# A two-layer encoder trunk on one core: 1488 of its 512-column products read their columns in another order

## The chip, the cores and the metric

The kernel runs on one core of a Trainium2 chip. The metric is the device time of one execution in microseconds (us), smaller is better. The engines are named as in the profile: PE is the matrix engine, PEld its weight loads, DVE the vector engine, ACT the scalar engine, POOL the general engine, SP the engine that issues most transfers. A PE product has a stationary operand of 128 by 128 values (its weight load) and a moving operand of 128 partitions by up to 512 columns, and it adds into a bank of 512 fp32 columns in PSUM.

## The reference

The reference is a trunk of two layers over 512 tokens of width 1024, batch 1, in float32. Layer A mixes by a matrix memory (4 heads) beside memory cross-attention, layer B by banded attention (12 heads) beside memory cross-attention. Each layer ends in an output projection and a gated MLP with a causal convolution. What bears on the change are these three places, in both layers:

```python
x = x + jnp.concatenate([mix_out, mem_out], axis=-1) @ w_out
u, g = jnp.split(h @ w_up, 2, axis=-1)          # D_FF = 2816 each
g = causal_dwconv(g, conv_w, conv_b)
return (jax.nn.silu(g) * u) @ w_down
```

The weights and the input are float32, and the result must agree with the float32 reference.

## The kernel before

Activations lie feature-major: a tile holds 128 features on the partitions and all 512 tokens on its columns. Every float32 operand is split into a high part (rounded to the fast fp32r type, by ACT, L140) and a low part (the rest, by DVE, L141). One float32 product of 128 by 128 weights with 512 tokens is three PE products, made by `mm3` (L192 to L196): high weights with high tokens, high weights with low tokens, low weights with high tokens, all into one PSUM bank. Since `mm3` records them, nearly all products of the kernel carry the lines L194, L195 and L196 in the profile, and the tiles tell them apart: `pmm`, `psc` and `ptr` are PSUM banks of the three tags "mm", "sc" and "tr" (3, 3 and 2 banks), `u` are tiles of 512 columns that hold split activations, `wh` and `wl` the split weights, `fh` and `fl` split forms of the weights in the MLP.

Weight tiles come from `weight_tiles` (L160). Two of its three pairs of buffers are 16 columns (`HALF`) longer than 1024, and one tile of such a pair begins 16 columns into its buffer (L167 to L171).

The products that the change touches are of 512 columns each, and contiguous in the columns before it:

- `project` (L198) makes one tile of 128 output features from 8 input tiles, so 24 PE products. It is called from many places; the change gives an order only to the calls in `ChannelMixer.plain` (L757), the gate and the up half of the first `PLAIN` = 5 tiles of each MLP: 5 tiles by 2 halves by 24 products by 2 layers = 480. The gate goes to a `pmm` bank, the up half to `psc`.
- `OutProjection.part` (L695) adds a few of the 8 mixed tiles at a time into 3 `pmm` banks and 2 banks of another tag (`ptr` in layer A, `psc` in layer B), as filler beside the last heads of the mixers: 5 banks by 8 tiles by 3 products by 2 layers = 240. The other 3 output tiles are made by `project` in `finish` (L708) and stay as they are.
- `ChannelMixer.down_products` (L822) multiplies one group of `GROUP` = 4 hidden tiles into one 128-row piece of the MLP's output, in a `ptr` bank: 32 pieces by 12 products by 2 layers = 768. ACT copies the bank to SBUF (L833) and a POOL transfer adds it to the spilled residual in DRAM (L834).

After the 5 plain tiles, each remaining MLP tile is made by `step` (L882) from seven blocks of products with 256 columns (`products`, L847), and its order on PE, ACT and DVE is written out by hand; up to two calls of `down_products` stand in one step. In the mixers, `weave` (L225) interleaves a job (a head of attention) with a filler (projections), at a rate written beside each call.

Of the kernel before, what the change touches and what calls it, by code (L numbers as in the profile page):

```python
# [16 lines left out]
P = 128  # L17
D = 1024
S = 512
KT = D // P  # L20
# [7 lines left out]
DFF = 2816  # L28
# [14 lines left out]
PLAIN, UNSCALED, GROUP, LAST = 5, 3, 4, 6  # L43
# [11 lines left out]
def trunk(  # L55
# [34 lines left out]
    def sb(tag, shape, dtype=F32):  # L90
        count[0] += 1
        return pool.tile(shape, dtype, tag=tag, name=f"{tag}{count[0]}", bufs=bufs[tag])

    def ps(tag):
        count[0] += 1
        return psum.tile([P, S], F32, tag=tag, name=f"p{tag}{count[0]}", bufs=pbufs[tag])
# [88 lines left out]
    def weights(*args):  # L185
        return parts(load(*args))

    def rows(w, c0, n, k0=0, k1=None):
        k1 = k1 if k1 is not None else w.shape[0] // P
        return w[k0 * P : k1 * P, c0 : c0 + n].rearrange("(k p) c -> p k c", p=P)  # L190

    def mm3(o, lh, ll, rh, rl, first, last, more=False):  # L192

        nc.tensor.matmul(o, lh, rh, start=first, stop=False, skip_group_check=more)  # L194
        nc.tensor.matmul(o, lh, rl, start=False, stop=False, skip_group_check=more)  # L195
        nc.tensor.matmul(o, ll, rh, start=False, stop=last, skip_group_check=more)  # L196

    def project(w, c0, act, tag="mm"):  # L198


        n = len(act)
        wh, wl = weights(rows(w, c0, P), n, P)
        o = ps(tag)
        for k in range(n):
            mm3(o, wh[:, k, :], wl[:, k, :], act[k][0], act[k][1], k == 0, k == n - 1)
            yield
        return o

    def run(gen):
        while True:  # L210
            try:
                next(gen)
            except StopIteration as end:
                return end.value

    def chain(*gens):
        for g in gens:
            yield from g

    def pair_of(a, b):  # L220
        first = yield from a
        second = yield from b
        return first, second

    def weave(job, filler, each, lead=0):  # L225

        due = lead
        for n in chain([0], job):
            due += each if n is None else each * n
            while due >= 1:  # L230
                due -= 1
                next(filler, None)
# [43 lines left out]
    class Norm:  # L276


        def __init__(self):
            self.acc = self.row = None  # L280
# [110 lines left out]
    def value_products_by_parts(os_, wh, wl, k0):  # L391

        n = wh.shape[1]
        for part, w in ((0, wh), (1, wh), (0, wl)):
            for k in range(n):
                for m, o in enumerate(os_):
                    a = memT[k0 + k][part][:, m * P : (m + 1) * P]
                    first = k0 + k == 0 and part == 0 and w is wh
                    nc.tensor.matmul(o, a, w[:, k, :], start=first, stop=w is wl and k0 + k == KT - 1)
# [63 lines left out]
    with tc.manual_schedule(engines={mybir.EngineType.PE, mybir.EngineType.Activation, mybir.EngineType.DVE}):  # L463

        logarithms()
        w = ps("mm")
# [39 lines left out]
        first, second = slice(0, MEM), slice(MEM, S)  # L506
# [13 lines left out]
        for q in range(KT // 2):  # L520
            k = 2 * q
# [166 lines left out]
    class OutProjection:  # L688


        def __init__(self, w, mixes, *groups):
            self.w, self.mixes, self.o = w, mixes, {}
            self.groups, self.n = groups, [0] * len(groups)

        def part(self, g, *ks):  # L695
            j0, j1, tag = self.groups[g]
            if j0 not in self.o:
                self.o.update((j, ps(tag)) for j in range(j0, j1))
            cols = slice(j0 * P, j1 * P)
            wh, wl = weights([self.w[k * P : (k + 1) * P, cols] for k in ks], len(ks), (j1 - j0) * P)  # L700
            for i, k in enumerate(ks):
                self.n[g] += 1
                for j in range(j0, j1):
                    c = slice((j - j0) * P, (j - j0 + 1) * P)
                    mm3(self.o[j], wh[:, i, c], wl[:, i, c], *self.mixes[k], self.n[g] == 1, self.n[g] == KT)
                    yield

        def finish(self, gnames):  # L708
# [12 lines left out]
    class ChannelMixer:  # L721
# [35 lines left out]
        def plain(self, j):  # L757
            scale = self.norm.row if j < UNSCALED else None
            act = self.act if j < UNSCALED else self.ready
            gate = project(self.w, DFF + j * P, act)  # L760
            up = project(self.w, j * P, act, "sc")
            if self.norm.row is None:
                both = pair_of(gate, up)
                weave(self.norm.finish(), both, 1)
                og, ou = yield from both
                scale = self.norm.row
            else:
                og = yield from gate
                ou = None
            acc = sb("t", [P, S])  # L770
            src = og
            if scale is not None:
                src = sb("t", [P, S])
                V.tensor_tensor(out=src, in0=og, in1=scale, op=ALU.mult)
            self.last_tap(j, acc, src)
            for _ in self.taps(j, acc, src):
                pass
            A.activation(acc, acc, AF.Silu)
            if scale is not None:
                V.tensor_mul(acc, acc, scale)  # L780
            if ou is None:
                ou = yield from up
            V.tensor_tensor(out=acc, in0=ou, in1=acc, op=ALU.mult)
            self.keep(acc)
# [37 lines left out]
        def down_products(self, u):  # L822
            g, j = divmod(u, KT)
            w = self.down[u // 2]
            o = ps("tr")
            c = slice(u % 2 * P, (u % 2 + 1) * P)
            for k in range(GROUP):
                mm3(o, w[0][:, k, c], w[1][:, k, c], *self.hid[GROUP * g + k], k == 0, k == GROUP - 1)
            return j, o

        def add(self, j, o):
# [211 lines left out]
    act = acts  # L1043
# [6 lines left out]
    def value_columns(hf):  # L1050
        n = AW // 2
        os_ = [ps(t) for t in ("mm", "mm", "mm", "sc")]
        for u in range(4):
            if hf:

                wh, wl = vw.pop()
                for j in range(2 * u + 2, min(2 * u + 4, KT)):
                    if j < KT - 1:
                        x_scaled(j + 1)
                    x_low(j)  # L1060
                    if j == 2 * u + 2:
                        vw.append(parts(value_weights(1, u + 1), pinned=True))
            else:
                wh, wl = parts(value_weights(0, u))
            nn = wh.shape[-1]
            for i in range(2):
                k = 2 * u + i
                for T in range(TT):
                    lh, ll = (t[:, T * P : (T + 1) * P] for t in act[k])
                    mm3(os_[T][:, :nn], lh, ll, wh[:, i, :], wl[:, i, :], k == 0, k == KT - 1)  # L1070
                    yield
        for T in range(TT):
            if hf:
                V.tensor_add(gt[:, T, :], os_[T][:, n : n + 8], gateb)
            hi, lo = sb("u", [P, S], F32R), sb("u", [P, S], F32R)
            G.memset(f(hi)[:, DH : DH + P], 1.0)
            G.memset(f(lo)[:, DH : DH + P], 0.0)
            split(pair(hi), pair(lo), os_[T][:, :n].rearrange("p (a b) -> p a b", a=2))
            vh[hf][T], vl[hf][T] = hi, lo
# [3 lines left out]
    e, u, c, r = (cpool.tile([P, TT, AH], F32, name=f"gate{i}") for i in range(4))  # L1083
# [7 lines left out]
    order = [(h, s) for h in range(AH) for s in range(TT)]  # L1091
# [80 lines left out]
    mixes = [None] * KT  # L1172
# [114 lines left out]
                mixes[j] = sb("u", [P, S], F32R), sb("u", [P, S], F32R)  # L1287
            split(mixes[j][0][r, :], mixes[j][1][r, :], og[j][r, :])

    outp = OutProjection(a_w_out, mixes, (0, 3, "mm"), (3, 5, "tr"))  # L1290
    run(value_columns(1))
    load_vectors(1)
    load_vectors(2)
# [44 lines left out]
    norm2, kvact, act = Norm(), [], []  # L1338
    for j in range(KT):
        wh, wl = weights(rows(ffn_w_down[0], j * P, P, FT - LAST, FT), LAST, P)  # L1340
        o = ps("mm")
# [10 lines left out]
    mixes = [None] * KT  # L1352
# [94 lines left out]
    def b_memory_queries(hp):  # L1447
        memq[hp] = queries((yield from project(b_w_in, AW + hp * P, act)), norm.row)

    qkv = {}  # L1450
    outp = OutProjection(b_w_out, mixes, (0, 3, "mm"), (3, 5, "sc"))
    fill = chain(*(project_pair(j) for j in range(5)), b_memory_queries(0), project_pair(5), b_memory_queries(1))
    weave(norm.finish(), fill, 1)
    for j in range(4):
# [65 lines left out]
    n = LAST // 2  # L1520
    for hf in range(2):
        os_ = [ps(t) for t in (("mm", "mm", "mm", "sc") if hf == 0 else ("sc", "sc", "tr", "tr"))]
        ws = [None] * n
        groups = [(range(TT), (slice(0, S),))]
        if hf:

            groups = [((0, 1), (slice(0, S),)), ((2,), (slice(0, S),)), ((3,), (slice(0, MEM), slice(MEM, S)))]
        for Ts, pieces in groups:
            for c in pieces:
                if c.start:  # L1530
                    os_[Ts[0]] = ps("mm")
                for u in range(n):
# [3 lines left out]
                    wh, wl = ws[u]  # L1536
                    for T in Ts:
                        for i in range(2):
                            k = 2 * u + i
                            lh, ll = (t[:, T * P : (T + 1) * P] for t in hid[k])  # L1540
# [57 lines left out]
```

## Time and profile before

| | us |
|---|---|
| median of 2 runs | 1178.32 |
| lowest and highest run | 1177.98, 1178.65 |
| span of the profiled execution | 1177.3 |
| PE busy (share) | 1167.7 (99%) |
| PEld busy (share) | 1033.3 (88%) |
| DVE busy (share) | 940.7 (80%) |
| ACT busy (share) | 728.5 (62%) |
| POOL busy (share) | 129.2 (11%) |

The span runs from the first to the last instruction of the profiled execution. A product's busy time in the profile overlaps the next product's, because products are pipelined; how often PE can start one is read from the start times in the timeline, not from the busy times. A group in the list of groups gives line, engine, operation, tiles and shapes, its count, its busy time in us and the mean of one in ns.

### The profile page before, as it was taken

How to read it: one execution, taken by the hardware profiler on the slowest of the kernel's cores; microseconds unless marked ns; L12 is line 12 of the kernel's file. 1: busy time of each engine (PE TensorE's matmuls, PEld its weight loads, DVE VectorE, ACT ScalarE, POOL GpSimd, SP SyncE). 2: the span in 40 equal slices, each digit the busy share in tenths (PEclk: the TensorE clock that was granted, in tenths of full speed). 3: DMA queues.
4: the chain of work that ended last, by engine and by line, in shares of the span. 5: the costliest groups of instructions: out<-in, count | busy, mean ns of one | idle time of the engine just before them, and what ended most of it. 6: DMA issues, size and time to landing. Idle time of an engine off the chain costs nothing.

```text
span 1177.3 us, 18645 instructions
## 1 busy us (share of the span) xinstructions
PE 1167.7 (99%) x7005; PEld 1033.3 (88%) x7005; DVE 940.7 (80%) x1680; ACT 728.5 (62%) x1297; POOL 129.2 (11%) x222
## 2 busy tenths in 40 slices
PE   9999999999999999999999999999999999999997
PEld 9988888888889999999888888778889999999986
DVE  6777788887979888777688888897897887777755
ACT  6548677655656655666666677676565666666545
POOL 1211101000021111111020000101001011110100
PEclk9999999999999999999999999999999999999999
DMA  8645325243366766665563312335426456666551
GB/s 277 230 111 140 86 55 152 76 144 116 90 159 159 181 166 165 167 147 118 154 204 117 90 54 89 112 89 179 142 90 152 108 138 142 143 144 144 126 161 72
DMA packets 199277, 158.64 MB, mean 135 GB/s; under 512 B 8361, under 2 KB 178063, under 8 KB 199187
## 3 DMA queue, kind: packets, MB, share of 16 engines
q1 hardware_dynamic: 183026, 119.74, 34.5%
q0 software_dynamic: 15584, 36.67, 15.6%
q8 instruction: 55, 0.90, 0.3%
q10 hardware_dynamic: 576, 1.05, 0.2%
q14 instruction: 36, 0.29, 0.1%
HBM read 128.89 MB, written 32.46 MB: 137 GB/s over the span
## 4 chain that ended last, share of the span: by engine, by line
PE 95%; ACT 2%; DVE 2%; issue 0%; POOL 0%; POOLq 0%; DVEq 0%; ACTq 0%
PE pmm L194 18%; PE pmm L195 18%; PE pmm L196 18%; PE ptr L195 6%; PE ptr L194 6%; PE ptr L196 6%; PE psc L196 5%; PE psc L195 5%; PE psc L194 5%; PE psc L600 2%; PE ptr L1421 1%; PE ptr L1442 1%; PE ptr L1443 1%; PE ptr L669 0%; PE pmm L491 0%; PE pmm L470 0%
## 5 line engine op out<-in xcount | busy, mean ns | idle before, releaser
L194 PE MATMUL pmm<-u,wh 128*128 128x512 f32 (+1 forms) x968 | 333.2, 345 | 0.2 <-ACT u L140 0.2
L196 PE MATMUL pmm<-u,wl 128*128 128x512 f32 (+1 forms) x968 | 330.6, 342 | 0.0
L195 PE MATMUL pmm<-u,wh 128*128 128x512 f32 (+1 forms) x968 | 330.4, 342 | 0.0
L141 DVE TENSOR_TENSOR wl<-wr,wh 128x1024 fp32r<-128x1024 f32 (+3 forms) x172 | 199.7, 1162 | 82.4 <-ACT wh L140 80.9
L140 ACT CAST wh<-wr 128x1024 fp32r<-128x1024 f32 (+3 forms) x172 | 171.9, 1002 | 91.5 <-PE pmm L195 41.0
L196 PEld LDWEIGHTS pmm<-u,wl 128*128 128x128 f32 x968 | 181.8, 188 | 20.8
L194 PEld LDWEIGHTS pmm<-u,wh 128*128 128x128 f32 x968 | 181.8, 188 | 18.5 <-ACT u L140 1.1
L195 PEld LDWEIGHTS pmm<-u,wh 128*128 128x128 f32 x968 | 182.0, 188 | 18.1 <-DVE u L141 0.5
L194 PE MATMUL ptr<-u,wh 128*128 128x512 f32 x272 | 106.4, 391 | 0.0
L195 PE MATMUL ptr<-u,wh 128*128 128x512 f32 x272 | 106.2, 390 | 0.0
L196 PE MATMUL ptr<-u,wl 128*128 128x512 f32 x272 | 105.8, 389 | 0.0
L834 POOL DMA_DIRECT2D xspill<-t x64 | 55.5, 867 | 429.7 <-ACT t L833 417.2
L890 ACT COPY t<-pmm 128x256 f32<-128x256 f32 x102 | 38.0, 372 | 76.7 <-PE pmm L196 76.5
L141 DVE TENSOR_TENSOR u<-t,u 128x512 fp32r<-128x512 f32 (+1 forms) x94 | 54.1, 596 | 35.4 <-ACT u L140 35.4
L194 PE MATMUL pmm<-u,fh 128*128 128x256 f32 x272 | 75.4, 277 | 0.0
L194 PE MATMUL psc<-u,wh 128*128 128x256 f32 (+1 forms) x232 | 75.3, 324 | 0.0
L195 PE MATMUL pmm<-u,fh 128*128 128x256 f32 x272 | 75.2, 276 | 0.0
L196 PE MATMUL pmm<-u,fl 128*128 128x256 f32 x272 | 75.1, 276 | 0.0
L196 PE MATMUL psc<-u,wl 128*128 128x256 f32 (+1 forms) x232 | 75.1, 324 | 0.0
L195 PE MATMUL psc<-u,wh 128*128 128x256 f32 (+1 forms) x232 | 74.9, 323 | 0.0
L141 DVE TENSOR_TENSOR fl<-pt,fh 128x512 fp32r<-128x512 f32 x102 | 70.3, 689 | 5.1 <-ACT fh L140 1.4
L140 ACT CAST fh<-pt 128x512 fp32r<-128x512 f32 x102 | 62.9, 616 | 8.9 <-DVE pt L944 5.5
(352 smaller groups left out, 2495.9 us busy)
## 6 DMA issues: line engine op xcount, KB each, us to landing
wr<-in_ffn_w_up_dram SPq DMA_DIRECT2D x54, 512.0 KB, 6.1
wr<-in_ffn_w_down_dram SPq DMA_DIRECT2D x38, 512.0 KB, 5.1
pt<-in_ffn_w_up_dram SPq DMA_DIRECT2D x34, 512.0 KB, 7.7
xspill<-t POOLq DMA_DIRECT2D x64, 256.0 KB, 4.3
wr<-in_a_w_in_dram SPq DMA_DIRECT2D x20, 512.0 KB, 3.8
wr<-in_w_kv_dram SPq DMA_DIRECT2D x12, 512.0 KB, 4.1
xspill<-fh POOLq DMA_DIRECT2D x16, 256.0 KB, 2.8
xspill<-fl POOLq DMA_DIRECT2D x16, 256.0 KB, 2.9
```

Source lines behind the costliest of these rows:

```text
L140: high = A.copy(hi, src) if on_act else V.tensor_copy(hi, src)
L141: low = V.tensor_tensor(out=lo, in0=src, in1=f(hi), op=ALU.subtract)
L194: nc.tensor.matmul(o, lh, rh, start=first, stop=False, skip_group_check=more)
L195: nc.tensor.matmul(o, lh, rl, start=False, stop=False, skip_group_check=more)
L196: nc.tensor.matmul(o, ll, rh, start=False, stop=last, skip_group_check=more)
L600: nc.tensor.matmul(o, a, b, start=first and i == 0, stop=i == 1)
L834: G.dma_start(xspill[j], t, accum_op=ALU.add)
L890: A.copy(o, r[:, :H])
L1421: nc.tensor.transpose(tp[:, b * P : (b + 1) * P], es[T, h][:, b * P : (b + 1) * P], ident)
L1442: nc.tensor.matmul(o2[:, s * P :], w, hi_at(pts[h], s, s, TT - s), start=s == 0, stop=False)
L1443: nc.tensor.matmul(o2[:, s * P :], w, lo_at(pts[h], s, s, TT - s), start=False, stop=s == TT - 1)
```

## The change

`mm3` gets an optional `order`, a function that rewrites the access patterns of the PSUM output and of the moving operand in the same way. The stationary operand is not rewritten. Each column of the output still gets the product of the same column, so the values are the same; only the sequence in which one PE product goes through its 512 columns differs.

`blocks_of(n, e)` cuts the columns into `n` equal parts and reads a piece of `e` columns from each part in turn: with n = 2 and e = 16 the columns 0 to 15, 256 to 271, 16 to 31, 272 to 287 and so on. `backwards` reads from column 511 down to 0.

```diff
+    def blocks_of(n, e):
+        return lambda a: a.rearrange("p (h b e) -> p b h e", h=n, e=e)
+
+    def backwards(a):
+        n = a.shape[-1]
+        return bass.AP(tensor=a.tensor, offset=a.offset + n - 1, ap=[list(a.ap[0]), [-1, n]])
+
-    def mm3(o, lh, ll, rh, rl, first, last, more=False):
+    def mm3(o, lh, ll, rh, rl, first, last, more=False, order=None):
 
+        if order is not None:
+            o, rh, rl = order(o), order(rh), order(rl)
         nc.tensor.matmul(o, lh, rh, start=first, stop=False, skip_group_check=more)
...
-            gate = project(self.w, DFF + j * P, act)
-            up = project(self.w, j * P, act, "sc")
+            order = (blocks_of(2, 2), backwards)[self.l]
+            gate = project(self.w, DFF + j * P, act, order=order)
+            up = project(self.w, j * P, act, "sc", order=order)
...
-                mm3(o, w[0][:, k, c], w[1][:, k, c], *self.hid[GROUP * g + k], k == 0, k == GROUP - 1)
+                mm3(o, w[0][:, k, c], w[1][:, k, c], *self.hid[GROUP * g + k], k == 0, k == GROUP - 1,
+                    order=blocks_of((2, 4)[self.l], 16))
...
-    outp = OutProjection(a_w_out, mixes, (0, 3, "mm"), (3, 5, "tr"))
+    outp = OutProjection(a_w_out, mixes, blocks_of(2, 32), (0, 3, "mm"), (3, 5, "tr"))
...
-    outp = OutProjection(b_w_out, mixes, (0, 3, "mm"), (3, 5, "sc"))
+    outp = OutProjection(b_w_out, mixes, blocks_of(2, 4), (0, 3, "mm"), (3, 5, "sc"))
```

By place and order:

| place | order | products |
|---|---|---|
| plain tiles, layer A | 2 parts, pieces of 2 | 240 |
| plain tiles, layer B | backwards | 240 |
| down-projection, layer A | 2 parts, pieces of 16 | 384 |
| down-projection, layer B | 4 parts, pieces of 16 | 384 |
| output projection, layer A | 2 parts, pieces of 32 | 120 |
| output projection, layer B | 2 parts, pieces of 4 | 120 |

`project` and `OutProjection` hand the order through to `mm3`. No instruction is added or removed, and no transfer, tile, buffer or wait is changed.

More of the change, by code (lines that the diff above doesn't have):

```diff
@@ L196, in mm3, with project @@
         nc.tensor.matmul(o, ll, rh, start=False, stop=last, skip_group_check=more)
-    def project(w, c0, act, tag="mm"):
+    def project(w, c0, act, tag="mm", order=None):
         n = len(act)
@@ L204, in project @@
         for k in range(n):
-            mm3(o, wh[:, k, :], wl[:, k, :], act[k][0], act[k][1], k == 0, k == n - 1)
+            mm3(o, wh[:, k, :], wl[:, k, :], act[k][0], act[k][1], k == 0, k == n - 1, order=order)
             yield
@@ L688, in trunk, with __init__ @@
     class OutProjection:
-        def __init__(self, w, mixes, *groups):
-            self.w, self.mixes, self.o = w, mixes, {}
+        def __init__(self, w, mixes, order, *groups):
+            self.w, self.mixes, self.o, self.order = w, mixes, {}, order
             self.groups, self.n = groups, [0] * len(groups)
@@ L704, in part @@
                     c = slice((j - j0) * P, (j - j0 + 1) * P)
-                    mm3(self.o[j], wh[:, i, c], wl[:, i, c], *self.mixes[k], self.n[g] == 1, self.n[g] == KT)
+                    mm3(self.o[j], wh[:, i, c], wl[:, i, c], *self.mixes[k], self.n[g] == 1, self.n[g] == KT,
+                        order=self.order)
                     yield
```

## The prediction, made before the changed kernel had run

> **What bounds the kernel now.** I read the page first: the engines' busy shares, then the chain that ended last.
>
> ```profile
> span 1177.3 us, 18645 instructions
> ...
> PE 1167.7 (99%) x7005; PEld 1033.3 (88%) x7005; DVE 940.7 (80%) x1680; ACT 728.5 (62%) x1297; POOL 129.2 (11%) x222
> ...
> PEclk9999999999999999999999999999999999999999
> ...
> PE 95%; ACT 2%; DVE 2%; issue 0%; POOL 0%; POOLq 0%; DVEq 0%; ACTq 0%
> ```
>
> PE is busy for 99% of the span and makes 95% of the chain, at a granted clock of nine tenths or more throughout. The change adds and removes no instruction, so it can act on the time only through how fast PE goes through its columns. I therefore checked next, in the table of windows, that PE also sets the pace in the very stretches that hold the changed products: the plain tiles of layer A, the rest of its MLP, the last heads of layer B with the output projection, and the two stretches of layer B's MLP.
>
> ```profile
> core 0: us, PE busy (x) PEld busy (x) DVE busy (x) ACT busy (x) POOL busy (x), PEclk, DMA share, GB/s
> ...
> 258.00:340.00 82.00, 82.00 (x363) 67.70 (x362) 72.74 (x117) 48.87 (x78) 5.30 (x8) 1.00 0.41 119
> 340.00:575.00 235.00, 235.00 (x1735) 221.54 (x1734) 188.84 (x272) 141.49 (x238) 39.42 (x53) 1.00 0.65 155
> 766.00:812.00 46.00, 45.71 (x243) 37.07 (x243) 37.50 (x98) 32.33 (x77) 1.64 (x3) 1.00 0.39 114
> 834.00:895.00 61.00, 61.00 (x273) 50.56 (x272) 56.22 (x95) 37.62 (x61) 2.59 (x3) 1.00 0.38 105
> 895.00:1130.00 235.00, 235.00 (x1735) 221.54 (x1734) 189.35 (x272) 141.33 (x238) 24.70 (x29) 1.00 0.60 139
> ```
>
> In both MLPs PE never pauses, while DVE has 189 of 235 us and 73 of 82 us of work. A change of a few per cent in PE's pace goes straight into the time there. In the window of the output projection PE pauses for 0.3 us; part of what is won there would turn into longer waits for the heads' softmax.
>
> How many products are changed comes from the list of groups by shape (one of the three lines each) and from the code.
>
> ```profile
> L194 PE MATMUL pmm<-u,wh 128*128 128x512 f32 x544 | 216.1, 398 | 0.2 <-ACT u L140 0.2
> ...
> L194 PE MATMUL ptr<-u,wh 128*128 128x512 f32 x272 | 106.4, 391 | 0.0
> ...
> L194 PE MATMUL psc<-u,wh 128*128 128x512 f32 x96 | 37.7, 393 | 0.0
> ```
>
> All 272 into ptr (256 of the down-projection, 16 of layer A's output projection) and all 96 into psc (80 up halves, 16 of layer B's output projection) are changed; of the 544 into pmm 80 gates and 48 of the output projections. That is 496 a line, 1488 over the three lines.
>
> **The pace of one product.** The mean of 391 ns in those rows is pipelined; the pace is the distance of starts in the timeline. First a plain stretch of 512 columns, then the same three lines in a down-projection with the next product behind it.
>
> ```profile
> 261.81 0.39 PE L194 MATMUL pmm<-u,wh 128*128 128x512 f32 x1
> 262.03 0.39 PE L195 MATMUL pmm<-u,wh 128*128 128x512 f32 x1
> 262.26 0.39 PE L196 MATMUL pmm<-u,wl 128*128 128x512 f32 x1
> 262.49 0.39 PE L194 MATMUL pmm<-u,wh 128*128 128x512 f32 x1
> ...
> 264.98 0.39 PE L196 MATMUL pmm<-u,wl 128*128 128x512 f32 x1
> ```
> ```profile
> 901.25 0.40 PE L194 MATMUL ptr<-u,wh 128*128 128x512 f32 x1
> 901.25 0.19 PEld L195 LDWEIGHTS ptr<-u,wh 128*128 128x128 f32 x1
> ...
> 903.99 0.28 PE L194 MATMUL pmm<-u,fh 128*128 128x256 f32 x1
> ```
>
> The first and last row of the plain stretch are 14 products apart: 3.17 us / 14 = 226.4 ns. The down-projection's 12 products take 2.74 us, 228.3 ns each. The next product's weight load begins with each product, so PE reads two operands at once. Other shapes tell how much of the 226 ns is bare streaming: 384 columns, and 256 columns in two places.
>
> ```profile
> 56.27 0.33 PE L194 MATMUL pmm<-wh,u 128*128 128x384 f32 x1
> ...
> 59.05 0.33 PE L195 MATMUL pmm<-wl,u 128*128 128x384 f32 x1
> ...
> 59.39 0.27 PE L1119 MATMUL ptr<-ident,lf 128*4 128x128 f32 x1
> ...
> 59.94 0.27 PE L1120 MATMUL ptr<-ident,ic 128*4 128x128 f32 x1
> ```
> ```profile
> 899.88 0.28 PE L194 MATMUL pmm<-u,wh 128*128 128x256 f32 x1
> ...
> 901.13 0.28 PE L196 MATMUL pmm<-u,wl 128*128 128x256 f32 x1
> ```
> ```profile
> 30.73 0.28 PE L399 MATMUL pmm<-wh,u 128*128 128x256 f32 x1
> ...
> 33.13 0.28 PE L399 MATMUL pmm<-wh,u 128*128 128x256 f32 x1
> ```
>
> 384 columns: 16 products in 2.78 us, 173.8 ns. From there to 512 columns it is 52.6 ns for 128 columns, 0.411 ns a column, so 512 columns at that rate alone would be 210 ns, and 226.4 ns holds about 16 ns that aren't streaming. The same 256 columns run at 1.25 us / 11 = 113.6 ns in the MLP and at 2.40 us / 20 = 120.0 ns in the value products at L399. One shape, two paces, no wait in either: there is a step of 6.4 ns that depends on what is read and written beside what, not on the amount of work. The rows don't say whether it is the place of the operands in memory or the bank, which alternates at L399.
>
> **The change, part by part.** Nothing is moved between queues: SP, POOL, ACT and DVE issue what they did, and no wait is added. Three things can cost or win.
>
> The instruction itself: an access pattern with three steps instead of one. No row shows a product with such a pattern, so its issue is bounded by nothing and by the 16 ns that are not streaming now. I take nothing, since a product is issued while the one before it streams for over 200 ns; without that cover it would be up to 1488 x 16 ns = 24 us.
>
> The hops between pieces: no row shows a moving operand that hops. Bounds: nothing, or one column's time, 0.411 ns, at each piece. I take nothing: in the rows PE already goes from the end of one tile to the start of the next with each product, and all that it loses there, everything included, is 16 ns in 512 columns. The other end is the second rival's.
>
> The distance between the two reads: this is where the change can win. A weight load of 128 columns can't be repeated faster than the transposes above, 0.55 us / 5 = 110 ns, or 0.86 ns a column, half the rate of the moving operand. A contiguous moving read overtakes the weight load; a read in two parts advances in each part at half its rate, as fast as the load, and so keeps its distance. If the step of 6.4 ns is a meeting of the two reads, an order in parts takes one such step out of the two and a half in the 16 ns. The bounds for one product are 0 and 16 ns of gain (below nothing by the hops). I take 6.4 ns, the one step that the rows show to come and go, for the orders in parts, and nothing for the backwards reads, which meet the load whatever they do.
>
> [...]
>
> The sum: 480 - 240 backwards leaves 240 plain products, with 768 of the down-projection and 240 of the output projections 1248; 1248 x 6.4 ns = 8.0 us. All are on PE's chain. The profiled execution has 1177.3 us of span, and the median of the runs, 1178.3, is 1.0 us over it. 1177.3 - 8.0 + 1.0 = 1170.3 us. When PE gets faster, ACT's copy of the bank and the splits of the next weights are next in line: the 384 down-projection products of a layer win 2.5 us together, and DVE alone has 46 us to spare in the 235 us that hold most of them, so nothing is late there.
>
> **The rivals.**
>
> *No change.* The 16 ns belong to each 512-column product whatever the order. For it: in the plain stretch at 262 us the pace is the same for high and low weights, which begin at different columns of their buffers. Against it: the 6.4 ns between two paces of one shape. Time: 1178.3, with the scatter of the runs 1177 to 1180.
>
> *Slower by the hops.* Each piece costs one column's time. The pieces of one product are 256, 128, 32 and 16 for pieces of 2, 4, 16 and 32, and backwards each of 512 columns counts. 240 x 256 x 0.411 ns = 25.3 us, 240 x 512 = 50.5, 768 x 32 = 10.1, 120 x 16 = 0.8, 120 x 128 = 6.3: together 93 us, 1271 us. It is decided where 93 us shrinks to 2% of the time, 23.6 us: from 0.10 ns a piece, a quarter of a column, it is slower. For it: nothing in the trace excludes it. [...] Against it: no hop in a row has such a price, and each price paid between tiles is within the 16 ns.
>
> *All the excess goes.* Reads and loads never meet, backwards included: 1488 x 16 ns = 23.8 us, 1154.5 us. For it: 0.411 ns a column is reached between 384 and 512. Against it: no group of products in the trace runs without an excess; the best, 113.6 ns for 256 columns, still has 8 ns over 105.
>
> *Another engine becomes the bound.* DVE's 72.74 of 82.00 us is the fullest window; 240 x 6.4 ns = 1.5 us less for PE leaves it 7.7 us of spare. I give it no chance of its own.
>
> **How the numbers follow.** Forecast, some but not all of the excess goes: 0.57. No change: 0.22. Slower by the hops: 0.17, of which 0.12 beyond 2%. All the excess: 0.04, half of it beyond 2%. A difference of 2% is about what a measurement of this kernel can tell from no change. Faster by over 2% thus 0.02, slower 0.12, within 0.86. The likeliest time is 1170. The forecast's own range goes from all 16 ns on the 1248 products, 20.0 us, 1158, to a quarter of the 8.0 us, 1176; with the no-change case it becomes 1157 to 1180, which leaves out the hops and the full excess, about 2 in 10.
>
> **What would show it.** In the timeline of the changed kernel, the starts of down-projection products should stand 220 to 222 ns apart instead of 228, and those of the plain tiles of layer B 226 as before. The groups' counts and all other paces stay. 226 in every place would be the first rival; over 230 in the plain tiles, most of all backwards or in pieces of 2, the second. The forecast is wrong if PE's pace falls and the span doesn't, or if products with the same order differ more than products with different orders do.

## The result and the profile after

The changed kernel takes 1216.95 us (median; 1216.5 to 1217.4) against 1178.32 us before: the ratio is 1.032, with a 95% interval of 1.031 to 1.034. It is slower by 38.6 us, and the profiled execution by 37.5 us of span. The forecast of 1170 us and its range were both missed; what happened is the prediction's second rival, at less than half its size.

The first lines of the changed kernel's page, its engines' busy times and the chain that ended last:

```profile
span 1214.8 us, 18649 instructions
...
PE 1205.4 (99%) x7005; PEld 1037.6 (85%) x7005; DVE 942.8 (78%) x1680; ACT 729.5 (60%) x1297; POOL 129.2 (11%) x222
...
PEclk9999999999999999999999999999999999999999
...
PE 96%; ACT 2%; DVE 1%; issue 0%; POOL 0%; POOLq 0%; DVEq 0%; ACTq 0%
```

The same 7005 products are there, at the same granted clock (0.999 on average in both). The counts of the other engines' instructions are the same too (the four instructions more in the first line are none of theirs), their work has hardly grown (DVE by 2.1 us, ACT by 1.0), and PE is still busy for 99% of the span. So PE goes more slowly through the same columns. Where it does so is seen in the table of windows. The first line below is of the kernel before, from the first plain product of layer A to just past its last one (a first down-projection lies in the window too); the second is of the changed kernel over the same work.

```profile
274.00:331.80 57.80, 57.80 (x256) 47.63 (x256) 53.91 (x92) 35.93 (x58) 0.54 (x1) 1.00 0.30 90
```
```profile
274.20:358.80 84.60, 84.60 (x255) 50.01 (x254) 55.02 (x92) 35.51 (x58) 0.54 (x1) 1.00 0.22 66
```

After the span of the window stand the busy times of PE, PEld, DVE, ACT and POOL. DVE and ACT do the same number of instructions in about the same time, and the window is 26.8 us longer: five tiles hold 71% of the loss. In the timeline of the changed kernel, first a plain tile of layer A, then a down-projection of layer A with the next product behind it:

```profile
291.97 0.51 PE L204 MATMUL pmm<-u,wh 128*128 128x512 f32 x1
292.31 0.51 PE L205 MATMUL pmm<-u,wh 128*128 128x512 f32 x1
...
296.05 0.51 PE L204 MATMUL pmm<-u,wh 128*128 128x512 f32 x1
```
```profile
364.62 0.40 PE L204 MATMUL ptr<-u,wh 128*128 128x512 f32 x1
...
367.50 0.28 PE L204 MATMUL pmm<-u,wh 128*128 128x256 f32 x1
```

The plain products start 4.08 us / 12 = 340 ns apart, one and a half times the 226.4 ns of before, and the 12 products of the down-projection 2.88 us / 12 = 240 ns. Read in this way for all six places, from the start of each changed product to the start of the next one on PE (mean ns, and its growth times the count):

| place | order | products | before, ns | after, ns | added, us |
|---|---|---|---|---|---|
| plain tiles, layer A | 2 parts, pieces of 2 | 240 | 227.3 | 338.7 | 26.8 |
| plain tiles, layer B | backwards | 240 | 226.8 | 233.4 | 1.6 |
| down-projection, layer A | 2 parts, pieces of 16 | 384 | 227.7 | 240.1 | 4.8 |
| down-projection, layer B | 4 parts, pieces of 16 | 384 | 227.7 | 232.2 | 1.7 |
| output projection, layer A | 2 parts, pieces of 32 | 120 | 237.4 | 243.1 | 0.7 |
| output projection, layer B | 2 parts, pieces of 4 | 120 | 247.3 | 264.6 | 2.1 |

Together 37.6 us, which is all of the 37.5 us in the span. No place got faster. The products of 512 columns in the other projections, whose order the change leaves alone, stay as they were (234.4 and 234.5 ns, waits included).

### The profile page after: what moved, and what is told of

Its sections match the earlier page's. It is cut to its first block, busy times and chain, and to the rows that moved or that the text cites. A ratio compares the mean times of both kernels' runs of the same rounds, so it can differ in the third digit from the quotient of the medians.

```text
span 1214.8 us, 18649 instructions
## 1 busy us (share of the span) xinstructions
PE 1205.4 (99%) x7005; PEld 1037.6 (85%) x7005; DVE 942.8 (78%) x1680; ACT 729.5 (60%) x1297; POOL 129.2 (11%) x222
## 4 chain that ended last, share of the span: by engine, by line
PE 96%; ACT 2%; DVE 1%; issue 0%; POOL 0%; POOLq 0%; DVEq 0%; ACTq 0%
PE pmm L204 18%; PE pmm L205 18%; PE pmm L206 18%; PE ptr L205 6%; PE ptr L206 6%; PE ptr L204 6%; PE psc L206 5%; PE psc L205 5%; PE psc L204 5%; PE psc L610 2%; PE ptr L1434 1%; PE ptr L1455 1%; PE ptr L1456 1%; PE ptr L679 1%; PE pmm L501 0%; PE pmm L480 0%
## 5 line engine op out<-in xcount | busy, mean ns | idle before, releaser
L204 PE MATMUL pmm<-u,wh 128*128 128x512 f32 (+1 forms) x968 | 339.1, 351 | 0.1
L206 PE MATMUL pmm<-u,wl 128*128 128x512 f32 (+1 forms) x968 | 336.6, 348 | 0.0
L205 PE MATMUL pmm<-u,wh 128*128 128x512 f32 (+1 forms) x968 | 336.4, 348 | 0.0
L206 PE MATMUL ptr<-u,wl 128*128 128x512 f32 x272 | 108.6, 399 | 0.0
L205 PE MATMUL ptr<-u,wh 128*128 128x512 f32 x272 | 108.5, 399 | 0.0
L204 PE MATMUL ptr<-u,wh 128*128 128x512 f32 x272 | 108.3, 398 | 0.0
L204 PE MATMUL psc<-u,wh 128*128 128x256 f32 (+1 forms) x232 | 80.8, 348 | 0.0
L206 PE MATMUL psc<-u,wl 128*128 128x256 f32 (+1 forms) x232 | 80.5, 347 | 0.0
L205 PE MATMUL psc<-u,wh 128*128 128x256 f32 (+1 forms) x232 | 80.5, 347 | 0.0
```

## The experiments

The diffs are shortened to what each kernel changes. Where no number of executions is given, a kernel was executed once, and its paces come from that trace; the mean granted clock was between 0.998 and 1.0 in all of them.

**Do the places add up?** The changed kernel, but with layer A's plain tiles read straight; four executions.

```diff
-            order = (blocks_of(2, 2), backwards)[self.l]
+            order = (None, backwards)[self.l]
```

> All orders of the change but that of layer A's plain tiles, which read straight again. Theory P (the places add up, each product at its own pace): the 240 plain products go back from 339 ns to 227 ns, 26.8 us less than the changed kernel's 1217.0, so 1190 us, 1.0% over the kernel before. Theory Q (one slow place drags the others, by the weight splits or the copies that follow later): more than that goes, 1180 us or less. The paces of the other five places stay at 233 (backwards), 240 and 232 (down-projection), 243 and 265 (output projections) under P, and fall towards 227 under Q.

It took 1190.1 us, 1.010 times the kernel before (1.008 to 1.011), as theory P has it. The plain tiles of layer A were back at 227.5 ns and the other five paces within 0.3 ns of the changed kernel's. Each place pays for itself.

**Which side pays, the read or the write?** Two kernels: one gives the order to the moving operand alone, the other to the PSUM output alone. The other side goes straight through its columns, cut into as many steps so that the shapes agree.

```diff
-            o, rh, rl = order(o), order(rh), order(rl)
+            rh, rl = order(rh), order(rl)      # the other kernel: o = order(o)
```

> Only the moving operand is read in the change's orders; the PSUM output is written straight, so the 1488 products put their columns in the wrong places (the values of those columns are changed). If the price of an order is paid where the moving operand is read (theory M), the paces stay as in the changed kernel: 339 ns in layer A's plain tiles, 233 backwards, 240 and 232 in the down-projections, and the time near 1217 us. If it is paid where PSUM is written (theory W), all go back to 227 ns, and the time to about 1179 us. Backwards may be paid on the other side than the pieces.

> Only the PSUM output is written in the change's orders; the moving operand is read straight (the columns of the 1488 products are put in the wrong places). Theory W: 339 ns in layer A's plain tiles, 233 backwards, 240 and 232 in the down-projections, about 1217 us. Theory M: 227 ns everywhere, about 1179 us.

The groups of up-half and output products into `psc`, one of the three lines, with the order on the moving operand alone and then on the PSUM output alone (busy us, mean ns of one):

```profile
L215 PE MATMUL psc<-u,wh 128*128 128x512 f32 x96 | 43.3, 451 | 0.0
```
```profile
L215 PE MATMUL psc<-u,wh 128*128 128x512 f32 x96 | 37.7, 393 | 0.0
```

The changed kernel has 43.3 us and 451 ns in this row, the kernel before 37.7 and 393. The whole price is paid by the read: with the order on the read alone the kernel takes 1218.1 us and the paces are 338.7, 233.3, 240.1 and 232.2 ns; with the order on the write alone it takes 1179.2 us beside 1179.1 for the kernel before on that chip, and the paces are 227.0, 226.8, 227.7 and 227.7 ns, backwards and pieces of 2 included. Writing in pieces of 2 to 32, or backwards, cost nothing that the runs can tell.

**How does the price go with the length of the pieces?** Two parts, both operands, other lengths.

```diff
+    orders: plain tiles A blocks_of(2, 4), B blocks_of(2, 8); down-projection A blocks_of(2, 32), B blocks_of(2, 64)
```

> Two parts everywhere, both operands, with pieces of 4 in layer A's plain tiles, 8 in layer B's, 32 and 64 in the down-projections of layer A and B; the output projections read straight. Theory H (a fixed price a piece, 0.44 ns as pieces of 2 show): 128, 64, 16 and 8 pieces cost 57, 28, 7 and 4 ns, so 283, 255, 234 and 230 ns. Theory L (a read fetches a line of 4 columns, and only pieces shorter than a line pay): 227 ns at 4, 8, 32 and 64 alike, with at most the steps of 6.7 ns that pieces of 16 and 32 show already.

Neither theory held. Pieces of 4, 8, 32 and 64 took 250.1, 243.3, 236.7 and 227.8 ns. A fixed price a piece would be 283 for pieces of 4; that pieces of a line or more are free is not so either. There is a large price for pieces of 2 (338.7 ns in the changed kernel) and a small one that fades out at 64.

**Is it the place of the weights, as the prediction thought?** Two of three pairs of weight tiles swap their 16-column shift; layer A's plain tiles and the output projections read straight.

```diff
-            at = HALF if i < 2 and (block is None) == (tag == "wh") else 0
+            at = HALF if i < 2 and (block is None) != (tag == "wh") else 0
```

> The 16-column shift of two of the three pairs of weight tiles goes to the other tile of the pair (high for low and the reverse), so that for two pairs in three the weight loads lie 16 columns off where they lay against the moving tiles: what began alike for products of 512 columns is now one chunk of 64 bytes apart, and what was one chunk apart for the MLP's products of 256 columns now begins alike. Orders as in the change in the down-projections and backwards, straight in layer A's plain tiles and the output projections. Theory M (the moving read meets the next weight load where both lie alike): the 256-column products of the MLP go from 113.6 to 120 ns, about 84 x 6.4 ns a step, some 15 us in all; of the products in two parts, which keep the distance they begin with, those with shifted weights leave 240 ns, for 227 to 233. Straight 512 columns change by at most one step of 6.7 ns. Theory L (only the lengths of the pieces count): the down-projections stay at 240 and 232 ns, backwards at 233, and 256 columns at 113.6.

In the MLP of that kernel, products of 256 columns with weights from those pairs:

```profile
911.00 0.28 PE L215 MATMUL pmm<-u,wh 128*128 128x256 f32 x1
911.12 0.28 PE L216 MATMUL pmm<-u,wh 128*128 128x256 f32 x1
...
913.04 0.28 PE L217 MATMUL pmm<-u,wl 128*128 128x256 f32 x1
```

The products of 256 columns with weights from those pairs went from 113.6 to 2.04 us / 17 = 120.0 ns: the step of 6.4 ns in the prediction is real, and it is the place of the weights against the moving operand that makes it. But the orders do not care: the down-projections stayed at 240.1 and 232.4 ns, backwards at 233.3. Straight 512 columns in layer A's plain tiles went from 227.3 to 230.6 ns. So theory M's numbers came true for straight reads and not for reads in pieces. The kernel took 1202.8 us, beside 1179.4 for the kernel before on that chip.

**More parts, and falling blocks.** Two kernels.

```diff
+    parts: plain tiles A blocks_of(4, 2), B blocks_of(32, 2); down-projection A blocks_of(8, 16), B blocks_of(2, 16)
+    falling(e): ap = [[-e, 512 // e], [1, e]] from column 512 - e; e = 16, 32 in the plain tiles, 64, 128 in the down-projections
```

> Pieces of 2 from 4 parts (layer A's plain tiles) and from 32 parts (layer B's plain tiles), pieces of 16 from 8 parts (down-projection of layer A) and from 2 parts (layer B); both operands. Theory L: the length of a piece sets the price, so pieces of 2 take 340 ns with 4 and with 32 parts as with 2, and pieces of 16 take 240 ns with 8 parts. Theory M: with more parts the read leaves a bank sooner, so pieces of 16 fall to 233 or less with 8 parts, and 2 parts in layer B show the 240 that layer A had. Pieces of 2 below 300 ns in either place would speak against L.

> One run through the columns in blocks that fall: the last block of e columns first, each block read forwards. e = 16 in layer A's plain tiles, 32 in layer B's, 64 and 128 in the down-projections; the output projections straight. Theory L: whole lines are read, so all stay at 227 ns. Theory M: a falling read meets the load more often than a rising one, 233 ns as backwards shows at 16 and 32, and 227 at 128; it begins 64, 128, 256 and 512 bytes off the load, so one of them may also fall below 226.

The timeline of the kernel with more parts, in a plain tile of layer A:

```profile
291.82 0.62 PE L216 MATMUL psc<-u,wh 128*128 128x512 f32 x1
...
294.92 0.62 PE L217 MATMUL psc<-u,wl 128*128 128x512 f32 x1
```

Pieces of 2 from 4 parts take 3.10 us / 7 = 443 ns, nearly twice straight reading; from 32 parts 431 ns. So the 340 ns of two parts is the mild case, and length alone is not the rule. Two parts of 16 show 240.1 ns in layer B as in layer A: the place in the kernel doesn't matter. Eight parts of 16 took 238.7 ns, against theory M's 233. Falling blocks of 16 and 32 took 233.3 ns both, of 64 and 128 227.9 and 227.8: 32 hops that go back cost half of what 32 hops between two parts cost (13 ns), and nothing was faster than straight.

**The cost by itself.** 42 series of 16 products behind the kernel before, once to vary orders, weight loads and the shift, once to vary where the parts begin.

```diff
+    for c, (order, at, n, wide) in enumerate(CASES):
+        o = ps(("mm", "sc")[c % 2])
+        for i in range(16):
+            st = hid[i % 2][i // 2 % 2][:, i // 4 * P : i // 4 * P + wide]
+            nc.tensor.matmul(order(o[:wide, :n]), st, order(mv[:, at * 16 : at * 16 + n]), start=i == 0, stop=i == 15)
```

> The kernel before, and behind its last product 42 series of 16 products of their own, whose sums nobody reads; while they run the other engines are all but idle. Moving operand and weights begin at the same place of a 512-byte row, but for the series that shift the moving operand by 1 to 7 chunks of 16 columns. [...] Theory L (lines of 4 columns): each visit to a line costs the time of 4 columns, so pieces of 2 from 4 parts take about 440 ns with weight loads of 128 columns and of 32, and pieces of 4 and more take what straight reading takes. [...] Theory O (the other engines' reads and writes hold up the moving read): every excess falls here already with weights of 128 columns, since the other engines are idle.

In the timeline of the first of these kernels a row is one series; the distance to the start of the next row, over 16, is about its pace. The figures in the text leave out the first three distances of a series, in which the pace settles. In this order: 2 parts of 2, of 4, of 8 (and the start of the next); 4 parts of 2, of 4, of 16; then straight with 512 columns (and the start of the next); straight with 256 columns, unshifted and shifted by one chunk; and with weight loads of 32 columns, straight with 512 and 256 columns, 2 parts of 2, of 4, of 16, and 4 parts of 2 and of 16.

```profile
1174.40 5.59 PE L1580 MATMUL psc<-pt,u 128*128 128x512 f32 x16
1179.82 4.18 PE L1580 MATMUL pmm<-pt,u 128*128 128x512 f32 x16
1183.83 4.05 PE L1580 MATMUL psc<-pt,u 128*128 128x512 f32 x16
1187.73 4.00 PE L1580 MATMUL pmm<-pt,u 128*128 128x512 f32 x16
...
1202.65 7.29 PE L1580 MATMUL pmm<-pt,u 128*128 128x512 f32 x16
1209.76 4.45 PE L1580 MATMUL psc<-pt,u 128*128 128x512 f32 x16
1214.05 3.89 PE L1580 MATMUL pmm<-pt,u 128*128 128x512 f32 x16
...
1247.30 3.79 PE L1580 MATMUL pmm<-pt,u 128*128 128x512 f32 x16
1250.92 3.84 PE L1580 MATMUL psc<-pt,u 128*128 128x512 f32 x16
...
1276.83 2.07 PE L1580 MATMUL pmm<-pt,u 128*128 128x256 f32 x16
1278.73 2.05 PE L1580 MATMUL psc<-pt,u 128*128 128x256 f32 x16
...
1291.88 3.86 PE L1580 MATMUL pmm<-pt,u 128*32 128x512 f32 x16
1295.59 1.99 PE L1580 MATMUL psc<-pt,u 128*32 128x256 f32 x16
1297.41 5.39 PE L1580 MATMUL pmm<-pt,u 128*32 128x512 f32 x16
1302.63 4.11 PE L1580 MATMUL psc<-pt,u 128*32 128x512 f32 x16
1306.58 4.01 PE L1580 MATMUL pmm<-pt,u 128*32 128x512 f32 x16
1310.42 7.36 PE L1580 MATMUL psc<-pt,u 128*32 128x512 f32 x16
1317.61 3.89 PE L1580 MATMUL pmm<-pt,u 128*32 128x512 f32 x16
```

And the table of windows over the series, in which DVE, ACT and POOL do nothing:

```profile
1174.40:1325.00 150.60, 150.60 (x657) 105.38 (x655) 0.00 (x0) 0.00 (x0) 0.00 (x0) 1.00 0.01 4
```

With every other engine idle the paces are those of the kernels (inside a series: 340.0, 250.0, 243.3 and 240.0 ns for pieces of 2, 4, 8 and 16, 443.3 for 4 parts of 2, 233.2 backwards), so theory O falls. With weight loads of a quarter of the columns they are 326.7, 246.7 and 240.0 for pieces of 2, 4 and 16 and, for 4 parts of 2, 444.5, and straight 512 columns take 231.7 beside 226.7 with the full load. If the weight load of the next product held up the moving read, all of these would have come down; straight reading, pieces of 16 and 4 parts of 2 did not. A shorter weight load helps a little in three places: straight 256 columns without a shift go from 119.8 to 113.6 ns, pieces of 2 from two parts from 340.0 to 326.7, pieces of 4 from 250.0 to 246.7. Straight 512 columns shifted by 0 to 7 chunks took 226.7, 228.8, 232.8, 233.3, 227.5, 228.9, 232.8 and 233.3 ns, so no place was better than the unshifted one, which has the pace of the kernel. Straight 256 columns shifted by one chunk took 117.8 ns, not the 113.6 of the MLP's products, whose weights lie one chunk off their moving operand; 114.6, at 3 and at 7 chunks, was the least there.

**What is a line?** The second kernel of this kind.

```diff
+    two_parts(m, e, apart): ap = [[e, 256 // e], [apart, 2], [1, e]], from column at of mv
```

> The kernel before, and behind it 42 series of 16 products of their own, with weight loads of 128 columns. All read pieces of e columns from two parts in turn; what varies is the column that the first part begins at, and how far apart the parts are (256 columns in the change). Theory L (the read fetches aligned lines of 4 columns, and each visit to a line costs at most the time of 4 columns, 1.7 ns): pieces of 4 that begin 1 or 2 columns off a line touch two lines each and go from 250 to some 340 to 440 ns; pieces of 8 and 16 so shifted cost less, since 3 lines stand for 2 and 5 for 4; a straight read that begins off a line costs nothing. Pieces of 2 stay at 340 whatever the distance of the parts. Theory B (lines that follow one another are in different banks, and two parts at a distance of 256 columns put two visits to the same bank side by side): pieces of 4 and 16 lose their 23 and 13 ns over straight reading when the parts are 260, 264, 272 or 288 columns apart, and keep them at 320, 384, 512 or 1024 as soon as that is a whole turn of the banks. Without B the distance changes nothing. Under both no series is faster than the 226.7 ns of straight reading.

In this order: two parts of 4 that begin on a line of 4 columns, 1 column off it, 2 off; of 8 and of 16, 2 off; of 2, on the line, 1 off (and the start of the next).

```profile
1185.21 4.16 PE L1571 MATMUL pmm<-pt,u 128*128 128x512 f32 x16
1189.21 5.45 PE L1571 MATMUL psc<-pt,u 128*128 128x512 f32 x16
1194.47 5.59 PE L1571 MATMUL pmm<-pt,u 128*128 128x512 f32 x16
1199.89 5.82 PE L1571 MATMUL psc<-pt,u 128*128 128x512 f32 x16
1205.53 4.97 PE L1571 MATMUL pmm<-pt,u 128*128 128x512 f32 x16
1210.34 5.51 PE L1571 MATMUL psc<-pt,u 128*128 128x512 f32 x16
1215.68 5.49 PE L1571 MATMUL pmm<-pt,u 128*128 128x512 f32 x16
1221.00 5.47 PE L1571 MATMUL psc<-pt,u 128*128 128x512 f32 x16
```

Pieces of 4 go from 250.0 to 330.0 and 339.8 ns when they begin 1 or 2 columns off a line, pieces of 8 from 243.3 to 348.9, pieces of 16 from 240.0 to 300.0, while a straight read that begins 1, 2 or 3 columns off takes 236.7, 233.3 and 228.9, at most 10 ns more. Pieces of the same length, read as often, cost 60 to 106 ns more by where they begin: the read goes by aligned lines of 4 columns, 16 bytes, and pays when it visits a line again for the rest of its columns.

The price of a visit comes from 4 parts of 2: 256 visits where straight reading makes 128, 443.3 - 226.7 = 216.6 ns for 128 more, 1.69 ns each, close to the 1.64 ns that four columns take at the prediction's 0.411. Pieces of 8 and 16 off the line make 64 and 32 visits more than on it, 108 and 54 ns by that price, and cost 106 and 60. Two parts of 2, and pieces of 4 off the line in two parts, also make 128 visits more, but pay about half: 340 ns. A difference that fits is how soon the read comes back to the line it left: after one or two other lines in these, after three or more where it pays in full (three with 4 parts of 2 and with pieces of 8 off the line, five with pieces of 16). No run varies that by itself, and for so early a return the count of visits doesn't give the price: pieces of 2 that begin 1 column off a line make 256 visits more and still take 333.3 ns, as on the line in this kernel.

Theory B fell for most of the price. The distance of the parts changed pieces of 16 by nothing (240.0 to 240.3 ns from 260 to 1024 columns). Of the 23 ns of pieces of 4 it changed 11 at most: they took 249.8 to 251.1 ns at 256, 260, 320, 384, 512 and 1024, and 239.9 to 243.3 at the other distances that keep both parts on their lines. A distance of 258, which puts the second part off its lines, cost 330.0 again. What the rest of the small price is, 4 to 40 ns a product where whole lines are read in pieces, stays open: it is not the length of the weight load, not another engine, and for pieces of 16 not the distance.

**Do long pieces win anything?** All 1488 products in two parts of 128; ten executions.

```diff
+    every order blocks_of(2, 128)
```

> The change's 1488 products all read and write two parts in turn in pieces of 128 columns. Theory L, with the small price of short whole-line pieces: pieces this long are as good as straight, so every place is back at its pace of before (227 to 228 ns in the plain tiles and down-projections) and the time within 0.2% of the kernel before, near 1179 us. If a pattern of several steps cost something in itself, for each product, the time would be above that: 1488 x 6.7 ns, 10 us, for one step a product. If two parts won anything by their distance to the weight load, it would be below, by up to 10 us.

1178.8 us against 1179.0 beside it, a ratio of 1.0001 (0.999 to 1.001). The plain tiles and the down-projections ran at 226.8 and 227.7 ns, as before. A pattern of several steps cost nothing in itself here, and two parts won nothing.

## Why the prediction was wrong

*PE's pace goes straight into the time.* Right: the six places' paces add up to 37.6 us, and the span grew by 37.5. The count of 1488 was right, and so was the pace of 226 to 228 ns (the rows at 262 us are of the output projection's end, but the plain tiles ran at 227.3 and 226.8).

*The instruction itself costs nothing.* Right, by the run with pieces of 128.

*"The hops between pieces ... I take nothing."* This is the step that failed. Its reason was that PE goes from tile to tile with each product and loses at most 16 ns there. But a change of tile comes once in 512 columns, and between tiles the read loses no part of a line; nothing in that row bounds what a line costs that is fetched for two of its four columns. In its place the runs showed a read that goes by lines of 4 columns, where pieces of 2 come back to each line: 338.7 ns for 227.3, and 26.8 of the 37.6 us. The other end of the bound, one column's time a piece, came close there by luck: pieces of 2 cost 111 ns for 256 pieces, 0.44 ns a piece beside the 0.411 that the prediction worked out, but from four parts the same 256 pieces cost 216.6 ns, 0.85 each.

*The distance between the two reads, 6.4 ns a product won.* Wrong in its second half. The step of 6.4 ns does come from where the weights lie (113.6 and 120.0 ns in the run with the swapped shift, and 113.6 again with a short weight load), so reading it from two rows of one shape was sound. That the 16 ns of 512 columns are made of the same steps was a guess, and the short weight loads refute it: the excess stays without most of the load (231.7 ns). No order and no place that was tried ran faster than straight reading (226.7 ns in the series), and what the 16 ns are stays open. Backwards, forecast at no change, lost 6.6 ns. The rate of the weight load, 0.86 ns a column, was misread besides: the rows at 59 us have a stationary operand of 4 columns (128*4) and a moving one of 128, so they don't show how fast a load of 128 columns can be repeated.

*The rival "slower by the hops".* It came true, by the read and not by the write. Term by term, forecast and measured: 25.3 and 26.8 us for pieces of 2, 50.5 and 1.6 backwards, 10.1 and 6.5 for the two down-projections, 0.8 and 0.7 for pieces of 32, 6.3 and 2.1 for pieces of 4. The count of pieces was the wrong unit. Backwards has 512 of them but leaves no line early, and pieces of 4 are whole lines; only pieces of 2 break lines. Reading two columns of a line one after the other did not avert the price: pieces of 2 do that, and took 340 to 443 ns in place of 227.

*The chance.* Slower had 0.17. The trace of before showed no product with pieces, and its rows could not exclude the price of one column a piece; with a gain that rested on one step of another shape, that rival deserved at least as much as the forecast.

## What to carry to other kernels

In these runs a product's moving operand in SBUF was read by aligned 16-byte lines: in two parts, pieces of 4 took 250.0 ns a product where they begin on such a line, 330.0 and 339.8 where they begin 1 or 2 columns off it, and pieces of 2 340. Keep each run at least a whole line of 4 fp32 columns and on a line's start; runs of a few whole lines still cost 4 to 40 ns a product here. The order of long runs (64 columns and more) cost next to nothing (227 to 229 ns beside 227), and the orders in which PSUM was written cost nothing (226.8 to 227.7 ns, and 1179.2 us beside 1179.1). Where a product is about to do 256 times what no row of the trace shows it doing, bound the price by the unit that could be fetched, not by what one change of tile costs. And an excess over bare streaming (here some 16 ns of 226, an estimate from the paces of 384 and 512 columns) is not yet something to win: find what makes it before it is priced as a gain.

## What the runs showed that was not expected

- The PSUM side took all of these orders at the pace of before: 226.8 to 227.7 ns in the plain tiles and down-projections, written backwards, in pieces of 2, and in pieces of 16 from two or four parts.
- Pieces of 2 from two parts cost 340 ns, from four parts 443 ns, as if a line left one visit ago were partly still at hand and one left three visits ago not; no run tests that by itself.
- Four parts of whole lines (pieces of 4) took 267.2 ns against 250.0 for two parts and 246.7 for sixteen, so even whole lines have a price in pieces; its cause was not found.
- By where weights and moving operand lie against each other, 256-column products took 113.6 or 120.0 ns in the kernels, and straight 512-column products 226.7 to 233.3 in the series, in a pattern that repeats after 4 chunks of 64 bytes.
